# Feed-forward by token group: weights read once for all tokens, or three times in halves

## The chip, the core and the metric

The kernel runs on one core of a Trainium2 chip. The metric is the device time of one execution in microseconds. The kernel before takes 3298.15 us, the median of 3 runs (3295.02 to 3298.2).

A core has five engines that run beside each other, each with its own queue in program order: TensorE (PE, matrix products; its weight loads are shown as PEld), VectorE (DVE), ScalarE (ACT), GpSimd (POOL) and SyncE (SP), which here issues transfers. DMA engines move data between device memory (HBM) and the on-chip memories: SBUF, and PSUM, into which PE writes its sums. Engines wait for each other through semaphores.

## The reference

Two layers of a transformer-like step in float32, for 1024 prompt tokens and 32 sample tokens with 1024 features. Cut to what matters here:

```
def _sq_relu_mlp(h, w_up, w_down):
    return jnp.square(jax.nn.relu(h @ w_up)) @ w_down

for layer in range(2):
    mix = _ab_mixer(...) if layer % 2 == 0 else _s5_mixer(...)
    x = x + _rmsnorm(mix, g[1])
    x = x + _rmsnorm(_cross_attn(_rmsnorm(x, g[2]), ...), g[3])
    h = _rmsnorm(x, g[4])
    x = x + _rmsnorm(_sq_relu_mlp(h, w_up[layer], w_down[layer]), g[5])
```

The feed-forward maps 1024 features to 4096 hidden ones and back. Layer 0 mixes tokens by retention and forgetting attention, layer 1 by an S5 state-space layer, whose input is a product of the normed x with a 1024 x 1024 matrix (`w_in_c`).

## The kernel before, in words

Activations lie feature-major, features on the 128 partitions, tokens along the free axis, in three groups: g0 and g1 of 384 tokens, g2 of 256 + 32 = 288. Each large float32 product runs as three passes in fp32r over splits x = xh + xl and w = wh + wl: wh with xh, wh with xl, wl with xh (`mm3`).

A weight block of 128 x 1024 floats (512 KB) comes through `wload`: SP issues a transfer into a staging tile `wst` (2 buffers), ACT copies it to `wh` (line 139), and DVE subtracts to get `wl` (line 140); `wh` and `wl` have 4 buffers each. A block serves 8 x 3 = 24 products per token group.

The feed-forward (`mlp`) goes over 8 chunks of 512 hidden features. In each chunk four up blocks are loaded and multiplied for g0, g1 and g2 in turn; each result is evacuated (`evac_up`) by ACT (relu, line 1343), DVE (square, line 1344), ACT (high half `ho`, line 1346) and POOL (low half, line 1347). Then four down blocks are loaded and give 8 outputs for each group, summed up over the chunks in `y` by DVE (line 1366). Each weight block is loaded once and serves 72 products. In the last chunk a group's `y` is complete; `done` then starts its `update`: sums of squares (ACT `sq` line 244, POOL `acc` line 245), their sum over partitions by a small product on PE (`c` or `a`), the reciprocal root (`ms`, `rc`, `r`), its spread over partitions by another small product (`b`), and then for each of 8 parts y times gain and root (`upd`, DVE line 273), plus the residual `xr` read back from HBM (line 274, on DVE or POOL), the stored copy `xs`, and the split of the new x for the next product (`xh` ACT line 201, `xl` DVE line 202). The cross-attention's output product before the feed-forward ends in the same `update`.

The order of PE's program is written by hand (`_Order`): `po.later` puts a small product off until enough other products stand before it, and `po.tick` inserts those that are due. The other engines are ordered by a scheduler, with evacuations and put-off pieces at a raised priority; each engine then takes its instructions strictly in that order.

After the feed-forward of layer 0 comes the S5 input product: `gemm` over 8 blocks, the first `gran` of them taken together per token group before the next group, and each finished block goes to `s5_block`, whose first products on PE use a table `Gm`. PSUM has three banks for large products (`mm`).

## Time and profile before

| | |
|---|---|
| median of the runs | 3298.15 us (3295.02 to 3298.2) |
| span of the profiled execution, first to last instruction | 3296.3 us |
| instructions | 50246 |
| PE, PEld, DVE, ACT, POOL busy | 96%, 93%, 45%, 33%, 28% |
| mean granted clock of TensorE | 0.980 |
| DMA | 285.71 MB, mean 87 GB/s |

The profile is of one execution. Its own time is not listed apart from the runs; its span lies 1.9 us below their median. A granted clock of 1.00 is full speed. A matrix product's record is longer than its distance to the next, since products are pipelined: the distance between two starts is what counts.

### The profile page before, as it was taken

Reading aid. Unit: us, or ns where it says so; the run is one execution under the profiler, and the core shown is the slowest. Engines: PE = TensorE matmul, PEld = TensorE weight load, DVE = VectorE, ACT = ScalarE, POOL = GpSimd, SP = SyncE. Lnnn points to the kernel's source line nnn. Section 1 sums busy time; section 2 is a strip of 40 time slices with the busy share of each in tenths; the row PEclk is TensorE's granted clock in tenths of the full one; section 3 lists DMA queues with packets and bytes.
Section 4 is the critical chain, followed back from the end, with each engine's and each line's share of the span. In section 5 each row is a group of like instructions: output and inputs, shape, how many; then the busy total and the mean of one; then the engine's idle time right before and its main releaser. Section 6 shows DMA issues by size and latency. Waiting matters only on the chain.

```text
span 3296.3 us, 50246 instructions
## 1 busy us (share of the span) xinstructions
PE 3160.3 (96%) x19972; PEld 3059.2 (93%) x19972; DVE 1495.2 (45%) x2756; ACT 1071.6 (33%) x2117; POOL 914.5 (28%) x1182
## 2 busy tenths in 40 slices
PE   7999999998999999999999888998999999999997
PEld 7899986688999999999999878998999999999997
DVE  8843566527435223332334797227426132233224
ACT  5212335425435322221124334225435321222212
POOL 4873431216115211111114442015106111111115
PEclk9999999999999999999999998999999999999998
DMA  5562244124114211110112677114124110111113
GB/s 157 156 194 70 62 137 128 38 58 141 52 42 128 65 42 52 52 47 31 52 52 74 204 241 222 57 52 141 49 66 124 52 47 32 52 52 52 39 58 99
DMA packets 176336, 285.71 MB, mean 87 GB/s; under 512 B 34027, under 2 KB 130508, under 8 KB 175972
## 3 DMA queue, kind: packets, MB, share of 16 engines
q1 hardware_dynamic: 132310, 215.02, 21.8%
q10 hardware_dynamic: 35328, 41.83, 3.8%
q0 software_dynamic: 8464, 25.66, 2.3%
q8 instruction: 157, 2.57, 0.3%
q14 instruction: 77, 0.63, 0.1%
HBM read 220.17 MB, written 66.39 MB: 87 GB/s over the span
## 4 chain that ended last, share of the span: by engine, by line
PE 77%; DVE 7%; POOL 6%; DMA 4%; issue 4%; ACT 2%; SPq 0%; DVEq 0%; ACTq 0%; POOLq 0%
PE mm L72 68%; PE a L72 4%; PE b L72 2%; POOL q L527 2%; POOL acc L245 2%; PE c L72 1%; DVE xl L202 1%; DVE wl L140 1%; DVE upd L274 1%; POOL ET L528 1%; DMA ed<-ET 1%; POOL ET L529 1%; DVE upd L273 1%; PE b L76 1%; DMA mt<-in_memt_dram 0%
## 5 line engine op out<-in xcount | busy, mean ns | idle before, releaser
L72 PE MATMUL mm<-xh,wh 128*128 128x384 f32 (+1 forms) x3168 | 1050.4, 332 | 6.5 <-ACT mo L382 3.7
L72 PE MATMUL mm<-xh,wl 128*128 128x384 f32 (+1 forms) x3168 | 1031.4, 326 | 7.4 <-DVE wl L140 7.3
L72 PE MATMUL mm<-xl,wh 128*128 128x384 f32 (+1 forms) x3168 | 1031.9, 326 | 1.2 <-DVE xl L202 1.2
L72 PE MATMUL mm<-ho,wh 128*128 128x384 f32 (+1 forms) x3456 | 822.9, 324 | 1.5 <-DVE y L1366 1.5
L72 PEld LDWEIGHTS mm<-xh,wh 128*128 128x128 f32 x3168 | 603.5, 190 | 13.8 <-issue 5.0
L72 PEld LDWEIGHTS mm<-xh,wl 128*128 128x128 f32 x3168 | 602.4, 190 | 9.0 <-DVE wl L140 9.0
L72 PEld LDWEIGHTS mm<-xl,wh 128*128 128x128 f32 x3168 | 603.5, 190 | 1.8 <-DVE xl L202 1.8
L72 PEld LDWEIGHTS mm<-ho,wh 128*128 128x128 f32 x3456 | 603.5, 188 | 1.8 <-DVE y L1366 1.8
L72 PE MATMUL mm<-ho,wl 128*128 128x384 f32 (+1 forms) x1728 | 558.2, 323 | 0.0
L1347 POOL TENSOR_TENSOR ho<-u,ho 128x384 fp32r<-128x384 f32 (+1 forms) x192 | 183.3, 955 | 1176.2 <-ACT ho L1346 1150.4
L140 DVE TENSOR_TENSOR wl<-wst,wh 128x1024 fp32r<-128x1024 f32 (+1 forms) x252 | 318.5, 1264 | 416.0 <-ACT wh L139 412.8
L139 ACT ACTIVATE wh<-wst 128x1024 fp32r<-128x1024 f32 (+1 forms) x252 | 266.5, 1059 | 708.9 <-PE mm L72 641.6
L245 POOL TENSOR_TENSOR acc<-acc,sq 128x384 f32<-128x384 f32 (+2 forms) x259 | 280.9, 1093 | 412.1 <-ACT sq L244 406.5
L1366 DVE TENSOR_TENSOR y<-y,mm 128x384 f32<-128x384 f32 (+1 forms) x336 | 174.3, 519 | 353.4 <-PE mm L72 353.2
L72 PEld LDWEIGHTS mm<-ho,wl 128*128 128x128 f32 x1728 | 325.5, 188 | 0.0
L1344 DVE TENSOR_TENSOR u<-u 128x384 f32<-128x384 f32 (+1 forms) x192 | 103.3, 538 | 409.7 <-ACT u L1343 409.7
L1343 ACT ACTIVATE u<-mm 128x384 f32<-128x384 f32 (+1 forms) x192 | 88.0, 458 | 313.8 <-PE mm L72 313.6
L1346 ACT ACTIVATE ho<-u 128x384 fp32r<-128x384 f32 (+1 forms) x192 | 95.7, 498 | 172.1 <-DVE u L1344 172.1
L1206 POOL TENSOR_SCALAR p<-p,mx 128x256 f32<-128x256 f32 (+1 forms) x72 | 36.7, 510 | 241.4 <-DVE mx L1205 138.8
L202 DVE SCALAR_TENSOR_TENSOR xl<-upd,gall,xh 128x384 fp32r<-128x384 f32 (+1 forms) x120 | 100.0, 834 | 5.1 <-ACT xh L201 4.8
L244 ACT ACTIVATE sq<-y 128x384 f32<-128x384 f32 (+1 forms) x126 | 61.9, 495 | 109.7 <-DVE y L1366 56.2
L72 PE MATMUL mm<-xo,wh 128*128 128x384 f32 (+1 forms) x384 | 92.1, 324 | 0.0
(427 smaller groups left out, 4132.9 us busy)
## 6 DMA issues: line engine op xcount, KB each, us to landing
wst<-in_wup_dram SPq DMA_DIRECT2D x64, 512.0 KB
wst<-in_wdn_dram SPq DMA_DIRECT2D x64, 512.0 KB
xs<-upd ACTq DMA_DIRECT2D x80, 192.0 KB
xr<-xs SPq DMA_DIRECT2D x80, 192.0 KB
wst<-in_wab_dram SPq DMA_DIRECT2D x20, 512.0 KB
wst<-in_wxk_dram SPq DMA_DIRECT2D x16, 512.0 KB
wst<-in_wxv_dram SPq DMA_DIRECT2D x16, 512.0 KB
wst<-in_wxq_dram SPq DMA_DIRECT2D x16, 512.0 KB
```

The source lines that it names most:

```text
L72: return nc.tensor.matmul(out, lhsT, rhs, **kw)
L139: act(wh[:, :n], st[:, :n], AF.Copy)
L140: vtt(wl[:, :n], st[:, :n], wh[:, :n].bitcast(F32), op=SUB)
L202: stt(l, src, gain, h.bitcast(F32), op0=MULT, op1=SUB)
L244: act(sq[:, :n], src, AF.Square)
L245: return gtt(acc[:, :n], acc[:, :n], sq[:, :n], op=ADD)
L527: gtt(o[:, :, :, :m], ET[:, :, :, :m], a_, op=MULT)
L1343: act(t, ps, AF.Relu)
L1344: vtt(t, t, t, op=MULT)
L1346: act(h, t, AF.Copy)
L1347: gtt(lo, t, h.bitcast(F32), op=SUB)
L1366: vtt(Y[g][o], Y[g][o], ps, op=ADD)
```

## The change

The feed-forward takes the token groups one after the other. For each group it goes over 4 chunks of 1024 hidden features: 8 up blocks, then 8 outputs from 4 pairs of down blocks (8 hidden blocks are summed in PSUM before one evacuation, where it were 4), so `y` is summed up over 4 chunks. Each weight block is loaded once per group, three times in all, and serves 24 products per load. A group's `update` is issued when its own pass is over. PE's products are the same in number and shape.

`wload` stages each block in two halves of 128 x 512 floats (256 KB): two transfers, four half-sized `wst` buffers, two `wh` copies (line 141) and two `wl` subtractions (line 142). This holds for all of the kernel's weights. The S5 input product opens with three blocks instead of two. Comments are left out in the new file, so that line numbers shift (update: 273 becomes 275, 274 becomes 276, `xl` 202 becomes 204, `xh` 201 becomes 203, relu 1343 becomes 1355, square 1344 becomes 1356, the high half, now `hm`, 1346 becomes 1358).

```
@@ wload
-            st = wp.tile([128, 1040], F32, tag="wst", bufs=2, name="wst")
-            dma(st[:, :n], src.rearrange("p k m -> p (k m)"))
             wh = wp.tile([128, 1040], F32R, tag="wh", bufs=4, name="wh")
             wl = wp.tile([128, 1040], F32R, tag="wl", bufs=4, name="wl")
-            with tc.high_priority(offset=offset):
-                act(wh[:, :n], st[:, :n], AF.Copy)
-                vtt(wl[:, :n], st[:, :n], wh[:, :n].bitcast(F32), op=SUB)
+            src = src.rearrange("p k m -> p (k m)")
+            for s in (slice(0, n // 2), slice(n // 2, n)):
+                st = wp.tile([128, 520], F32, tag="wst", bufs=4, name="wst")[:, : n // 2]
+                dma(st, src[:, s])
+                with tc.high_priority(offset=offset):
+                    act(wh[:, s], st, AF.Copy)
+                    vtt(wl[:, s], st, wh[:, s].bitcast(F32), op=SUB)
@@ mlp
-            Y = [[None] * 8 for _ in range(3)]
-            for c in range(8):
-                H = [[None] * 4 for _ in range(3)]
...
-                gemm(range(4), lambda b: wload(A["wup"][l, 4 * c + b], 8, HP if c == 0 and b == 2 else 0), lambda g, k: get(X, g)[k], evac_up, 4)
-                ws = [wload(A["wdn"][l, c, s], 4) for s in range(4)]
-                for g in range(3):
...
+            for g in range(3):
+                n = NG[g]
+                Y, acc = [None] * 8, None
+                x = get(X, g)
+                for c in range(4):
+                    H = [None] * 8
+                    for b in range(8):
+                        wh, wl = wload(A["wup"][l, 8 * c + b], 8)
+                        ps = bank()[:, :n]
+                        for k in range(8):
+                            s = slice(k * 128, k * 128 + 128)
+                            mm3(ps, wh[:, s], wl[:, s], x[k][0], x[k][1], k == 0, k == 7)
                             po.tick()
                         with tc.high_priority(offset=HP):
...
+                            act(t, ps, AF.Relu)
+                            vtt(t, t, t, op=MULT)
+                            h, lo = (hid[0].tile([128, 384], F32R, tag="hab", bufs=16, name="hm")[:, :n] for _ in range(2))
+                            act(h, t, AF.Copy)
+                            gtt(lo, t, h.bitcast(F32), op=SUB)
+                            H[b] = (h, lo)
+                    if c == 3:
+                        acc = acc_tile(n)
+                    for s4 in range(4):
+                        ws = [wload(A["wdn"][l, 2 * c + j, s4], 4) for j in range(2)]
+                        for o in (2 * s4, 2 * s4 + 1):
+                            ps = bank()[:, :n]
+                            for k in range(8):
+                                wh, wl = ws[k // 4]
...
+                                mm3(ps, wh[:, s], wl[:, s], H[k][0], H[k][1], k == 0, k == 7)
+                                po.tick()
+                            with tc.high_priority(offset=HP):
+                                if c == 0:
+                                    Y[o] = ytile(g)
+                                    act(Y[o], ps, AF.Copy)
+                                else:
+                                    vtt(Y[o], Y[o], ps, op=ADD)
+                                if c == 3:
+                                    sumsq(acc, Y[o], n, o == 0, "sqa")
+                done(g, Y, acc)
@@ S5 input product
-        gemm(range(8), ..., evac_u, lambda at: 2 if at == 0 else 1,
+        gemm(range(8), ..., evac_u, lambda at: 3 if at == 0 else 1,
```

The first place is DVE at the entry of layer 0's feed-forward. In the kernel before, `wl_12040` is the low half of up block 1, `wl_12046` that of block 2 (block 0's stands three rows ahead of the first row here), `u_12114` the square of block 0, and `upd`, `xl` and `y` belong to g1's update.

```order
L202 SCALAR_TENSOR_TENSOR xl_12007<-upd_12003,gall_81,xh_12006 128x384
L274 TENSOR_TENSOR upd_12086<-upd_12086,xr_12084 128x384
L273 SCALAR_TENSOR_TENSOR upd_12127<-y_11685,gall_81,b_11928 128x384
L140 TENSOR_TENSOR wl_12040<-wst_12037,wh_12039 128x1024
L202 SCALAR_TENSOR_TENSOR xl_12065<-upd_12061,gall_81,xh_12064 128x384
L212 TENSOR_SCALAR ms_12107<-c_12103 128x3
L274 TENSOR_TENSOR upd_12127<-upd_12127,xr_12125 128x384
L140 TENSOR_TENSOR wl_12046<-wst_12043,wh_12045 128x1024
L202 SCALAR_TENSOR_TENSOR xl_12090<-upd_12086,gall_81,xh_12089 128x384
L273 SCALAR_TENSOR_TENSOR upd_12152<-y_11741,gall_81,b_11928 128x384
L1344 TENSOR_TENSOR u_12114<-u_12114 128x384
```

In the change `wl_12304` is the low half of up block 0, `wl_12380` that of block 1, and `u_12372` the square of block 0; the `upd` and `xl` ahead of it belong to g1's update.

```order
L204 SCALAR_TENSOR_TENSOR xl_12323<-upd_12319,gall_81,xh_12322 128x384
L276 TENSOR_TENSOR upd_12395<-upd_12395,xr_12393 128x384
L275 SCALAR_TENSOR_TENSOR upd_12420<-y_12013,gall_81,b_12200 128x384
L204 SCALAR_TENSOR_TENSOR xl_12348<-upd_12344,gall_81,xh_12347 128x384
L276 TENSOR_TENSOR upd_12420<-upd_12420,xr_12418 128x384
L142 TENSOR_TENSOR wl_12304<-wst_12309,wh_12303 128x512
L204 SCALAR_TENSOR_TENSOR xl_12399<-upd_12395,gall_81,xh_12398 128x384
L204 SCALAR_TENSOR_TENSOR xl_12424<-upd_12420,gall_81,xh_12423 128x384
L214 TENSOR_SCALAR ms_12365<-c_12361 128x3
L1356 TENSOR_TENSOR u_12372<-u_12372 128x384
L142 TENSOR_TENSOR wl_12380<-wst_12381,wh_12379 128x512
L142 TENSOR_TENSOR wl_12380<-wst_12385,wh_12379 128x512
```

Block 0's second half (`wst_12309`) now stands behind the add of g1's seventh part, and block 1's two halves behind block 0's square; before, blocks 1 and 2 stood ahead of that square. Block 0's first half stands nine rows ahead of its second.

The second place is ACT. In the kernel before, `wh_12039` (block 1) and then `wh_12045` (block 2) are made far ahead of block 0's relu `u_12114`; the rows up to that relu are these.

```order
L280 DMA xs113_118<-upd_12061 128x384
L139 ACTIVATE wh_12045<-wst_12043 128x1024
L244 ACTIVATE sq_12069<-upd_12061 128x384
L201 ACTIVATE xh_12089<-upd_12086,gall_81 128x384
L280 DMA xs114_119<-upd_12086 128x384
L244 ACTIVATE sq_12094<-upd_12086 128x384
L1343 ACTIVATE u_12114<-mm_12055 128x384
L201 ACTIVATE xh_12130<-upd_12127,gall_81 128x384
L280 DMA xs115_120<-upd_12127 128x384
```

In the change the high half of block 1, `wh_12379`, comes right behind block 0's relu `u_12372`.

```order
L282 DMA xs116_121<-upd_12420 128x384
L246 ACTIVATE sq_12428<-upd_12420 128x384
L1355 ACTIVATE u_12372<-mm_12313 128x384
L141 ACTIVATE wh_12379<-wst_12381 128x512
L141 ACTIVATE wh_12379<-wst_12385 128x512
L1358 ACTIVATE hm_12375<-u_12372 128x384
L141 ACTIVATE wh_12477<-wst_12479 128x512
L141 ACTIVATE wh_12477<-wst_12483 128x512
```

Block 1's high half moved from ahead of block 0's relu to behind it.

The third place is ACT where layer 0 goes over from g1 to g2. In the kernel before, g1's last parts (`xh_18775`, `xs217`) stand beside g2's first ones, and a weight that stands among them (`wh_19206`) is one of the S5 input product.

```order
L201 ACTIVATE xh_18775<-upd_18772,gall_81 128x384
L280 DMA xs216_145<-upd_18772 128x384
L244 ACTIVATE sq_18780<-upd_18772 128x384
L139 ACTIVATE wh_19206<-wst_19204 128x1024
L201 ACTIVATE xh_18800<-upd_18797,gall_81 128x288
L280 DMA xs220_147<-upd_18797 128x288
L241 ACTIVATE acc_18793<-upd_18797 128x288
L201 ACTIVATE xh_18811<-upd_18808,gall_81 128x384
L280 DMA xs217_146<-upd_18808 128x384
L244 ACTIVATE sq_18816<-upd_18808 128x384
```

In the change `u_18040` is the relu of g2's sixth up block (block 5), `wh_18047` the high half of the seventh (block 6), and `xh_18078` g1's last part.

```order
L1355 ACTIVATE u_18040<-mm_17989 128x288
L203 ACTIVATE xh_18032<-upd_18029,gall_81 128x384
L282 DMA xs216_145<-upd_18029 128x384
L1358 ACTIVATE hm_18043<-u_18040 128x288
L246 ACTIVATE sq_18037<-upd_18029 128x384
L203 ACTIVATE xh_18078<-upd_18075,gall_81 128x384
L282 DMA xs217_146<-upd_18075 128x384
L246 ACTIVATE sq_18083<-upd_18075 128x384
L141 ACTIVATE wh_18047<-wst_18049 128x512
L141 ACTIVATE wh_18047<-wst_18053 128x512
L141 ACTIVATE wh_18102<-wst_18104 128x512
```

The weight of the seventh block stands behind g1's last part and its square.

## Rows read from the trace of the kernel before

**Rows 1.** Busy time by engine, whole span: us, share, instructions.

```profile
PE 3160.3 (96%) x19972; PEld 3059.2 (93%) x19972; DVE 1495.2 (45%) x2756; ACT 1071.6 (33%) x2117; POOL 914.5 (28%) x1182
```

**Rows 2.** Table by stretch: length, busy time of each engine, clock, DMA share, GB/s.

```profile
core 0: us, PE busy (x) PEld busy (x) DVE busy (x) ACT busy (x) POOL busy (x), PEclk, DMA share, GB/s
1045.00:1080.00 35.00, 29.27 (x153) 28.41 (x153) 33.77 (x52) 20.84 (x44) 28.07 (x27) 0.85 0.69 201
1100.00:1780.00 680.00, 680.00 (x4237) 680.00 (x4236) 195.34 (x305) 159.95 (x270) 91.13 (x98) 1.00 0.15 47
1336.00:1345.00 9.00, 9.00 (x62) 9.00 (x61) 4.80 (x7) 2.12 (x2) 0.00 (x0) 1.00 0.47 152
1780.00:1860.00 80.00, 68.93 (x404) 67.97 (x403) 63.15 (x106) 36.46 (x72) 53.69 (x57) 0.87 0.59 180
2505.00:2550.00 45.00, 39.32 (x225) 38.21 (x224) 42.37 (x64) 26.57 (x56) 35.79 (x36) 0.89 0.59 174
```

**Rows 3.** Timeline of PE, layer 0's entry: start, length, operation, idle before and releaser.

```profile
1047.23 0.83 PE L72 MATMUL a<-ones_c,acc 128*128 128x1 f32 x6 [0.92 <-POOL acc L245]
...
1050.39 0.34 PE L72 MATMUL mm<-xh,wh 128*128 128x384 f32 x1
...
1053.86 0.34 PE L72 MATMUL mm<-xh,wl 128*128 128x384 f32 x1
1056.06 0.83 PE L72 MATMUL c<-ones_c,acc 128*128 128x1 f32 x6 [1.86 <-POOL acc L245]
...
1058.06 0.53 PE L72 MATMUL mm<-xl,wh 128*128 128x384 f32 x1
...
1071.45 0.51 PE L72 MATMUL mm<-xh,wl 128*128 128x384 f32 x1 [2.95 <-DVE wl L140]
...
1078.48 0.36 PE L72 MATMUL mm<-xh,wl 128*128 128x384 f32 x1
```

**Rows 4.** Timelines of DVE and ACT, the same entry.

```profile
1049.27 1.21 DVE L140 TENSOR_TENSOR wl<-wst,wh 128x1024 fp32r<-128x1024 f32 x1
1050.40 0.60 DVE L202 SCALAR_TENSOR_TENSOR xl<-upd,gall,xh 128x384 fp32r<-128x384 f32 x1
...
1053.84 1.51 DVE L140 TENSOR_TENSOR wl<-wst,wh 128x1024 fp32r<-128x1024 f32 x1
...
1055.21 1.06 ACT L139 ACTIVATE wh<-wst 128x1024 fp32r<-128x1024 f32 x1 [3.37 <-DMA wst<-in_wup_dram]
...
1058.62 1.36 DVE L202 SCALAR_TENSOR_TENSOR xl<-upd,gall,xh 128x384 fp32r<-128x384 f32 x1
...
1061.29 0.53 ACT L1346 ACTIVATE ho<-u 128x384 fp32r<-128x384 f32 x1 [2.74 <-DVE u L1344]
...
1061.71 0.55 DVE L274 TENSOR_TENSOR upd<-upd,xr 128x384 f32<-128x384 f32 x1
```

**Rows 5.** Timelines of PE, ACT, DVE and POOL, up blocks of 288 columns.

```profile
1472.28 0.29 PE L72 MATMUL mm<-xh,wl 128*128 128x288 f32 x1
...
1473.47 0.29 PE L72 MATMUL mm<-xh,wl 128*128 128x288 f32 x1
...
1474.24 0.39 ACT L1343 ACTIVATE u<-mm 128x288 f32<-128x288 f32 x1
1474.36 1.23 DVE L140 TENSOR_TENSOR wl<-wst,wh 128x1024 fp32r<-128x1024 f32 x1 [1.60 <-ACT wh L139]
...
1476.51 0.81 POOL L1347 TENSOR_TENSOR ho<-u,ho 128x288 fp32r<-128x288 f32 x1 [2.38 <-ACT ho L1346]
```

**Rows 6.** Waits of PE from 1790 to 1860: total us, times, longest.

```profile
PE b L72 <- POOL rc L220: 5.6, 2, 4.4
```

**Rows 7.** Timeline of PE: first S5 input product and first product with Gm.

```profile
1813.24 0.34 PE L72 MATMUL mm<-xh,wh 128*128 128x384 f32 x1
...
1869.99 0.39 PE L72 MATMUL a<-U,Gm 128*128 128x132 f32 x2
```

**Rows 8.** Chain of waits at the end of the kernel: start, length, what.

```profile
3269.56 1.40 POOL xt L274 x2
...
3277.33 1.45 PE c L72 x6
```

More of the change, by code (lines that the diff above doesn't have):

```diff
@@ L1360, in mlp @@
                             po.tick()
                         with tc.high_priority(offset=HP):
-                            if c == 0:
-                                Y[g][o] = ytile(g)
-                                act(Y[g][o], ps, AF.Copy)
-                            else:
-                                vtt(Y[g][o], Y[g][o], ps, op=ADD)
-                            if c == 7:
-                                sumsq(acc, Y[g][o], NG[g], o == 0, "sqa")
-                    if c == 7:
-                        done(g, Y[g], acc)
+                            t = npl.tile([128, 384], F32, tag="tmp", bufs=2, name="u")[:, :n]
@@ new lines, in mlp @@
+                            act(t, ps, AF.Relu)
[12 more added lines that the diff above has]
+                                wh, wl = ws[k // 4]
+                                s = slice((k % 4) * 256 + (o % 2) * 128, (k % 4) * 256 + (o % 2) * 128 + 128)
+                                mm3(ps, wh[:, s], wl[:, s], H[k][0], H[k][1], k == 0, k == 7)
[8 more added lines that the diff above has]
+                                    sumsq(acc, Y[o], n, o == 0, "sqa")
@@ L1513, in _body @@
         close_after(left, X, (0, 1), s5_start)
-        gemm(range(8), lambda b: wload(A["winc"][b], 8, HP if b < 2 else 0), lambda g, k: get(X, g)[k], evac_u, lambda at: 2 if at == 0 else 1,
+        gemm(range(8), lambda b: wload(A["winc"][b], 8, HP if b < 2 else 0), lambda g, k: get(X, g)[k], evac_u, lambda at: 3 if at == 0 else 1,
              post=lambda b, g: s5_block(b, uts.pop(b)) if un[b] == 3 else None, final=(2, 0, 1))
```

16 lines of the change are left out of this document (removed).

## The prediction, made before the change was timed

> **What bounds the kernel now.** I read the busy table first: TensorE (PE) is busy for 3160.3 of 3296.3 us [rows 1], so only a change in its work, its waits or its clock can move the time. The change adds no product and takes none away; what counts is where PE stands still or runs at half speed. The table by stretch comes next [rows 2]. In the long feed-forward stretch of layer 0 PE is busy for 680.00 of 680 us at clock 1.00: nothing can be gained there. Time is lost at three seams. From 1045 to 1080 (entry into layer 0's feed-forward) PE idles 5.73 us and runs at 0.85; with the missing clock charged on its busy time (0.15 x 29.27 = 4.4) that is 10.1 us. From 2505 to 2550 (the same entry in layer 1) it is 5.68 + 0.11 x 39.32 = 10.0 us. From 1780 to 1860 (the last chunk of layer 0 and the S5 input product) it is 11.07 + 0.13 x 68.93 = 20.0 us.
>
> The timeline of PE at the first entry [rows 3] shows how a seam costs. After an idle of 0.92 us the next products still start 0.17 us apart ((1053.86 - 1050.39) / 20 = 0.1735, so a block of 24 products takes 4.16 us with 384 columns; 21 of them cover 3.64 us). After 1.86 us idle the records lengthen, from 1058.06 on, from 0.34 to 0.53 us: the lower of the two clock levels (1.2 of 2.4 GHz). After 2.95 us they are long from 1071.45 to 1078.48, so of those 7 us nearly half, 3.2 us, is lost. The 2.95 us are a wait for `wl`, VectorE's low half of a weight: VectorE (DVE) is busy for 33.77 of the 35 us of this stretch [rows 2], with the norm updates of g1 and g2 in front of the weights.
>
> **Steady feed-forward: 0.** A weight block now serves 24 products, 3.17 us with 288 columns (24 x 0.132, from (1473.47 - 1472.28) / 9 [rows 5]), so the weight stream must triple to 512 KB per 3.2 to 4.2 us, 125 to 165 GB/s. Before already does that in bursts: from 1336 to 1345 PE is busy for 9.00 of 9 us at 152 GB/s, with the DMA engines busy for 0.47 of the time [rows 2]; 165 GB/s would be 0.51. Per block ScalarE (ACT) would need 2 half copies, a relu and a copy, DVE two halves and a square, all below 2.4 us of 3.2 or 4.2.
>
> The halves themselves: a whole `wl` takes 1.21 us and a whole `wh` 1.06 us [rows 4]. A 384-column add takes 0.55 us on DVE and a 384-column copy 0.53 on ACT [rows 4], so a line through the two points gives a 512-column half 0.68 and 0.64 us, two halves 1.36 and 1.28: 0.15 and 0.22 us more per block, beside PE's work in the steady stretches.
>
> **Hand-over from up to down: +2 us, between 0 and 8.** There are 24 of these, 3 groups x 4 chunks x 2 layers. The first down output needs the evacuation of the last up block after 21 products. Before shows that evacuation with 288 columns: relu at 1474.24, square behind a whole `wl`, copy, and POOL done at 1476.51 + 0.81 = 1477.32 [rows 5], 3.08 us. With a half `wl` (0.68 for 1.23) it is about 2.5, and a wait for the product's end and the semaphores come on top, against 2.8 us of cover (21 x 0.132); with 384 columns it is some 0.5 longer against 3.64 us. I take a quarter of a microsecond at the 8 of g2 and nothing at the 16 others; the top is 1 us at each of the 8. [...]
>
> **Entries: +12 us, between -2 and +26 for both.** Before, `wl` of block 0 ran at 1049.27 and of block 1 at 1053.84, with parts of g1's update behind them [rows 4]. The order of the change puts the first half of block 0 two update instructions later, and the second half behind the add of g1's seventh part of eight (the DVE pieces in the section on the change). The first is done at about 1051.4; then come eight instructions of 0.55 to 0.85 us, 6 us, and the half itself: 1058.1. PE, which could start at 1050.4, has used the first half by 1053.6: 4.5 us idle plus 0.9 before it, where before had 1.86. The clock then drops as it did after 2.95 us, 3.2 us, and I take 4 since a second wait follows. Block 1's `wh` stands on ACT behind the relu of block 0 (it was far ahead): relu, half `wh` and half `wl` end before its third product, about 2 us. Block 5 stands in the same way behind block 4 (another 2, plus 1.5 of clock), block 4's second half comes 0.7 late. Sum 0.9 + 4.5 + 4 + 2 + 2 + 1.5 + 0.7 = 15.6, plus the 0.92 that both have, 16.5 against 10.1: +6 each. The cover before was that the `wh` of three blocks stood ahead of block 0's relu. The low end is that the late halves take the place of before's waits altogether; the high end is block 2 or 3 caught as well (3 us and its clock).
>
> **Group switches: +12 us, between +4 and +22.** Before there was no such place: updates of g0 and g1 ran beside the down products of the next group, whose weights were there. Now g0's and g1's updates (8 parts of three instructions of 0.55 to 1.36 us [rows 4], some 16 us of DVE) run beside the first up blocks of the next group. In layer 0 the order puts block 5's second half of `wl` behind g0's whole update, and block 6's `wh` behind g1's whole update and block 5's relu (the ACT pieces of that section). The first is needed 20.8 + 2.1 us after the switch and comes at about 25: 2.5 idle and 1.5 of clock, 4 us. The second is needed at 6 x 3.17 = 19.0 and comes at 24: 5 idle and 2 of clock, 7 us. In layer 1 the last update has no split to make (stt and add alone): 0.5 us at each of its two switches, 1 in all. SP's queue matters too: g1's and g2's residual loads now stand among the weight loads, and one that waits for an update part holds the weights behind it; that is the top end.
>
> **Layer 0 into S5: -12 us, between -5 and -19.** At the end of layer 0 only g2's update is left. Before, PE waited there for POOL's `rc` alone 5.6 us [rows 6], with g1's update in the way. The feed-forward's last product is followed by one of S5's input at 1813.24, and the first `Gm` product starts at 1869.99 [rows 7], 56.8 us later. The change puts 195 products of 384 columns and 96 of 288 between them (165 and 72 before): 195 x 0.1735 + 96 x 0.132 + about 4 for the small ones + 2 of idle (two of three PSUM banks held by g2's evacuations) = 52.5. The 7 or so lost between 1780 and 1813 go as well. That makes 11 to 12. The S5 stage keeps its pace, set by its eight states. At the low end the third block's evacuation, which finds only two `u` buffers, costs 3 us at two groups; the high end is all of the 20.0.
>
> **Tail: -1 us (0 to -3).** POOL's residual adds of g1 (1.40 us at 3269.56) stand among the sums of g2, and the last norm product starts only at 3277.33 [rows 8]. They go; the chain of y, square and sum that is left is 2 us. **Halves elsewhere: 0 us (-4 to +6)**, 124 loads at +0.14, nearly all beside PE, some started earlier where the DMA ends last.
>
> Sum: 0 + 2 + 12 + 12 - 12 - 1 + 0 = +13 us. The profiled span is 3296.3, the median of the runs 3298.15; the 1.9 us around it stay. Forecast 3298.15 + 13 = 3311.
>
> **Rivals.** A, faster: the late half of block 0 takes the place of waits that are there anyway (the 1.86 us for `acc` lies inside it, and block 3, needed later, has its `wl` by then), and PE's short waits behind it keep the clock. Then the entries cost what they did (0), the switches 5, the hand-overs 0, and the S5 seam gives 18 and the tail 2: -15, 3283 us. For it: the 2.95 us at the entry and the 5.6 us at the seam [rows 3, 6] are owed to updates that stand ahead of more urgent work. Against it: each engine takes its instructions in the order printed, and there the second half of `wl` stands behind an update longer than the waits that it could hide. It decides once entries and switches together cost less than 13 us.
>
> B, no measurable change: the entries +6 together, the switches +8, the seam -14, the tail -1, so -1: 3297. For it: both sides rest on the same engine's queue and are of one size.
>
> C, much slower: the staged stream falls behind. The Trainium skill (DMA: Bandwidth & Descriptors, "Measured" and "Anatomy of one DMA") says to batch transfers to at least 1 MiB; these shrink to 256 KB, and by its fixed 2 us and 436 GB/s a half would take an estimated 2.6 us, a block 5.2 if its halves did not overlap, more than the 3.2 to 4.2 it may take. By the rows alone: if the 152 GB/s of the burst [rows 2] is all that the path gives, a block takes 524288 B / 152 GB/s = 3.45 us, 0.28 more than g2's 3.17; at 128 blocks of g2 that is 36 us on top of the sum: 3347. Against it: 0.47 busy in that burst.
>
> **Chances.** Forecast 0.50 (its own range 3304 to 3322), B 0.18, A 0.22, C 0.10. What can be told from no change here is 0.2%, 6.6 us: faster 0.22, same 0.18, slower 0.60. The bounds of the terms add to -24 and +57; 8 in 10 lies between 3283 and 3338.
>
> **What would show it.** In the table by stretch: 100% PE at clock 1.00 between the seams, about 150 GB/s. At the entries a wait for `wl` of 3 us or more some 12 products into the first up block, and waits for `wh` and `wl` at the starts of the second and the sixth; at both layer-0 switches one wait near block 5 or 6. The first `Gm` product should come 52 to 53 us after the last product of the feed-forward instead of 56.8. It is wrong if PE idles a little at each block (C), or if the entries lose no more than 10 us (A).

## The result and the profile after

The changed kernel takes 3358.77 us (median of 4 runs, 3352.57 to 3364.63) against 3298.18 for the kernel before: the ratio is 1.0182, 95% interval 1.0168 to 1.0197. The profiled execution spans 3354.8 us, 58.5 more than the 3296.3 before. The forecast was 3311, its range 3283 to 3338. The kernel is slower as forecast, but by 60.6 us where 13 were forecast: outside the range, and above even the 3355 to which the upper bounds of all terms add up.

The busy table of the kernel after (us, share, instructions):

```profile
PE 3172.4 (95%) x19972; PEld 3061.8 (91%) x19972; DVE 1751.9 (52%) x3328; ACT 1375.5 (41%) x2881; POOL 912.4 (27%) x1182
```

PE is busy for 12 us more than in [rows 1] with the same 19972 products, so part of the loss is time at the lower clock level; the rest is idle. Where it lies is read from the starts of seven products in the timeline of PE, which cut the program into stretches: the first up and the last down product of each layer's feed-forward, the first and the last product with `Gm`, and the first of the GLU stage (the gated product that ends layer 1's mixer). The table is worked out from them (us; each column is one profiled execution):

| stretch | before | after | difference |
|---|---|---|---|
| start to first up product of layer 0 | 1050.4 | 1055.4 | +5.0 |
| feed-forward, layer 0 | 762.7 | 790.8 | +28.1 |
| to the first Gm product | 56.9 | 52.0 | -4.9 |
| first to last Gm product | 131.5 | 130.2 | -1.3 |
| to the GLU stage (keys and values of the memory for layer 1's cross-attention) | 47.9 | 60.7 | +12.8 |
| GLU stage to first up product of layer 1 | 468.6 | 470.1 | +1.6 |
| feed-forward, layer 1 | 756.1 | 774.9 | +18.8 |
| tail | 22.2 | 20.7 | -1.6 |

The table by stretch of the kernel after (columns as in [rows 2]) shows that inside the feed-forward the losses sit where the prediction looked for them, and only there; the 12.8 us at the memory keys and the 5.0 ahead of the feed-forward lie outside it, where the prediction put nothing:

```profile
1055.00:1112.00 57.00, 43.21 (x216) 39.85 (x216) 44.27 (x69) 30.28 (x62) 30.80 (x30) 0.88 0.56 175
1115.00:1345.00 230.00, 230.00 (x1318) 230.00 (x1317) 93.90 (x156) 91.11 (x172) 30.75 (x31) 1.00 0.40 126
1345.00:1395.00 50.00, 44.89 (x255) 44.06 (x254) 36.90 (x55) 26.72 (x54) 24.52 (x22) 0.93 0.53 164
1395.00:1625.00 230.00, 230.00 (x1318) 230.00 (x1317) 93.88 (x156) 91.81 (x173) 30.92 (x31) 1.00 0.39 125
1625.00:1670.00 45.00, 35.35 (x247) 34.42 (x246) 34.59 (x55) 24.80 (x53) 21.52 (x22) 0.89 0.57 176
1670.00:1840.00 170.00, 169.61 (x1276) 168.90 (x1275) 85.41 (x151) 83.84 (x169) 23.21 (x29) 1.00 0.51 164
2559.00:2618.00 59.00, 44.98 (x219) 42.02 (x219) 45.24 (x69) 30.15 (x62) 31.15 (x31) 0.83 0.51 157
```

Between entry and switches PE is busy for 230 of 230 us at 126 and 125 GB/s, and with 288 columns for 169.61 of 170 at 164 GB/s with the DMA engines 0.51 busy: the stream keeps up. The entry (first row, and last row for layer 1) and the two switches (third and fifth) lose time.

Below, an up pass is a group's eight up blocks of one chunk, a down pass its eight outputs. Undisturbed, an up pass of the changed kernel takes 33.5 us with 384 columns and 25.5 with 288, a down pass 33.6 and 25.8.

The waits of PE at the entry of layer 0, from its timeline (in brackets: idle before, and releaser), which answer to [rows 3]:

```profile
1056.66 0.44 PE L72 MATMUL mm<-xh,wl 128*128 128x384 f32 x1 [0.77 <-DVE wl L142]
...
1064.72 0.69 PE L72 MATMUL mm<-xh,wl 128*128 128x384 f32 x1 [5.69 <-DVE wl L142]
...
1070.66 0.69 PE L72 MATMUL mm<-xh,wh 128*128 128x384 f32 x1 [1.10 <-ACT wh L141]
...
1089.25 0.44 PE L72 MATMUL mm<-xh,wl 128*128 128x384 f32 x1 [1.50 <-DVE wl L142]
...
1094.57 0.56 PE L72 MATMUL mm<-xh,wl 128*128 128x384 f32 x1 [2.94 <-DVE wl L142]
...
1099.10 0.44 PE L72 MATMUL mm<-xh,wh 128*128 128x384 f32 x1 [1.10 <-ACT wh L141]
```

These are the places that were named: block 0's two halves, block 1's `wh`, block 4, block 5's `wh`. The records of 0.69 us behind the long wait are products at the lower clock level (the granted clock is 0.50 from 1064.10 to 1074.20); those of 0.44 are the first after a wait of 0.77, 1.50 or 1.10 us at the higher one.

The waits at layer 0's two switches and at the memory keys, from the same timeline:

```profile
1377.12 0.69 PE L72 MATMUL mm<-xh,wh 128*128 128x384 f32 x1 [4.92 <-ACT wh L141]
...
1655.67 0.61 PE L72 MATMUL mm<-xh,wh 128*128 128x288 f32 x1 [8.12 <-ACT wh L141]
...
1994.82 0.58 PE L72 MATMUL mm<-xmh,wh 128*128 128x256 f32 x1 [13.16 <-ACT wh L141]
```

ACT's timeline before the second of them shows why `wh` is late: it stands behind the last square of g1's update.

```profile
1654.09 0.60 ACT L203 ACTIVATE xh<-upd,gall 128x384 fp32r<-128x384 f32 x1
1654.59 0.51 ACT L246 ACTIVATE sq<-upd 128x384 f32<-128x384 f32 x1
1655.01 2.18 ACT L141 ACTIVATE wh<-wst 128x512 fp32r<-128x512 f32 x4
```

### The profile page after: what moved, and what is told of

It is laid out like the page before. It is cut to its first block, busy times and chain, and to the rows that moved or that the text cites. A ratio compares the mean times of both kernels' runs of the same rounds, so it can differ in the third digit from the quotient of the medians.

```text
span 3354.8 us, 54104 instructions
## 1 busy us (share of the span) xinstructions
PE 3172.4 (95%) x19972; PEld 3061.8 (91%) x19972; DVE 1751.9 (52%) x3328; ACT 1375.5 (41%) x2881; POOL 912.4 (27%) x1182
## 4 chain that ended last, share of the span: by engine, by line
PE 77%; DVE 9%; DMA 4%; issue 4%; ACT 3%; POOL 2%; SPq 1%; DVEq 0%; ACTq 0%; POOLq 0%
PE mm L72 68%; PE a L72 4%; PE b L72 2%; PE c L72 1%; DVE wl L142 1%; DVE upd L276 1%; DVE xl L204 1%; DVE upd L275 1%; POOL acc L247 1%; PE b L76 1%; DMA U<-ud 1%; ACT wh L141 1%; DMA wst<-in_wxk_dram 1%; DVE u L1356 0%; DMA wst<-in_wdn_dram 0%
## 5 line engine op out<-in xcount | busy, mean ns | idle before, releaser
L142 DVE TENSOR_TENSOR wl<-wst,wh 128x512 fp32r<-128x512 f32 (+1 forms) x1016 | 702.0, 711 | 777.5 <-ACT wh L141 727.1
L141 ACT ACTIVATE wh<-wst 128x512 fp32r<-128x512 f32 (+1 forms) x1016 | 613.5, 627 | 796.5 <-PE mm L72 701.6
L72 PE MATMUL mm<-hm,wh 128*128 128x384 f32 (+1 forms) x3072 | 730.5, 323 | 4.1 <-ACT hm L1358 1.9
L72 PEld LDWEIGHTS mm<-xh,wh 128*128 128x128 f32 x3168 | 605.0, 191 | 37.5 <-ACT wh L141 20.0
L72 PEld LDWEIGHTS mm<-hm,wh 128*128 128x128 f32 x3072 | 535.1, 188 | 6.9 <-POOL hm L1359 4.4
L72 PE MATMUL mm<-hm,wl 128*128 128x384 f32 (+1 forms) x1536 | 494.9, 322 | 0.0
L1359 POOL TENSOR_TENSOR hm<-u,hm 128x384 fp32r<-128x384 f32 (+1 forms) x192 | 186.1, 970 | 1082.2 <-ACT hm L1358 1082.2
L72 PEld LDWEIGHTS mm<-hm,wl 128*128 128x128 f32 x1536 | 288.2, 188 | 0.0
L1377 DVE TENSOR_TENSOR y<-y,mm 128x384 f32<-128x384 f32 (+1 forms) x144 | 74.9, 520 | 163.6 <-PE mm L72 163.6
L1358 ACT ACTIVATE hm<-u 128x384 fp32r<-128x384 f32 (+1 forms) x192 | 95.7, 499 | 80.9 <-DVE u L1356 80.7
L246 ACT ACTIVATE sq<-y 128x384 f32<-128x384 f32 (+1 forms) x126 | 61.5, 492 | 109.9 <-DVE y L1377 60.9
L203 ACT ACTIVATE xh<-upd,gall 128x384 fp32r<-128x384 f32 (+1 forms) x120 | 69.8, 583 | 60.7 <-DVE upd L276 46.8
```

The source lines that it names most:

```text
L72: return nc.tensor.matmul(out, lhsT, rhs, **kw)
L141: act(wh[:, s], st, AF.Copy)
L142: vtt(wl[:, s], st, wh[:, s].bitcast(F32), op=SUB)
L203: act(h, src, AF.Copy, scale=gain)
L246: act(sq[:, :n], src, AF.Square)
L1358: act(h, t, AF.Copy)
```

## The experiments

The theories: **O**, the order on ACT and DVE puts weights behind updates, and that is the loss at entries and switches; **H**, the halves themselves cost outside the feed-forward; **G**, opening with three blocks costs later in the S5 stage; against O, **S** or **V**: the engines have no time for update and weights at once, in whatever order. Letters that come later are explained in the expectation that uses them. The stretches below are those of the table, against the kernel before.

**e1: halves alone.** The kernel before with the changed `wload`, nothing else.

```
-            st = wp.tile([128, 1040], F32, tag="wst", bufs=2, name="wst")
-            dma(st[:, :n], src.rearrange("p k m -> p (k m)"))
...
+            for s in (slice(0, n // 2), slice(n // 2, n)):
+                st = wp.tile([128, 520], F32, tag="wst", bufs=4, name="wst")[:, : n // 2]
...
```

> The kernel before with one part of the change alone: every weight block staged, copied and subtracted in two halves. The traces of before and after differ outside the feed-forward by +5.0 us up to the first up product (1050.4 to 1055.4) and by +12.8 us between the last Gm product and the first product of the GLU stage (47.9 to 60.7). Theory H (halves): both belong to the staging, so this kernel takes 3298 + 5 + 13, about 3312 to 3318, with the PE wait for wh of some 13 us at the memory keys. Theory G (three blocks opened): only the +5 belongs to the halves, so about 3303, and the memory keys keep their 48 us. The forecast on record put 0 on the halves elsewhere: 3298.

Measured: 3332.45 us, ratio 1.0101 (1.0084 to 1.0118): worse than any theory said. The stretches: +13.9 to the first up product, +8.8 and +8.2 in the feed-forwards, +3.2 at the memory keys. The wait of 13 us is not there, so that part of H falls. But the entry now shows the waits of the changed kernel, although all groups still share a weight (timeline of PE in e1):

```profile
1065.60 0.45 PE L72 MATMUL mm<-xh,wl 128*128 128x384 f32 x1 [0.78 <-DVE wl L142]
...
1073.64 0.69 PE L72 MATMUL mm<-xh,wl 128*128 128x384 f32 x1 [5.66 <-DVE wl L142]
...
1079.59 0.69 PE L72 MATMUL mm<-xh,wh 128*128 128x384 f32 x1 [1.10 <-ACT wh L141]
```

DVE's timeline in e1 has the two halves of block 0 with eight instructions of g1's update between them:

```profile
1064.63 0.92 DVE L142 TENSOR_TENSOR wl<-wst,wh 128x512 fp32r<-128x512 f32 x1
...
1072.11 1.48 DVE L142 TENSOR_TENSOR wl<-wst,wh 128x512 fp32r<-128x512 f32 x1
```

A weight in two pieces gives the scheduler room to put update parts between them, and the product needs both. In e1 the third block keeps the raised priority that `mlp` gives it before, and the change drops; the waits come all the same.

**e2: three opening blocks alone.**

```
-        gemm(range(8), ..., evac_u, lambda at: 2 if at == 0 else 1,
+        gemm(range(8), ..., evac_u, lambda at: 3 if at == 0 else 1,
```

> The kernel before with one part of the change alone: the S5 input product opens with three blocks. Theory G: PE spends its spare products earlier, so it runs out of them behind the last Gm product, +13 us there, and the first Gm product comes 4 to 8 us later after the feed-forward: 3306 to 3318. Theory H: the end of the S5 stage is paced by its states, so nothing is lost: 3296 to 3302, stretch from last Gm to the GLU stage 48 us.

Measured: 3319.77 us, ratio 1.0063 (1.0048 to 1.0078). +7.1 us to the first Gm product, +4.7 to the last, +7.3 behind it: theory G. The longest wait of PE from 1810 to 2060 (total, times, longest) is the one for `wh` at the memory keys, with whole blocks:

```profile
PE mm L72 <- ACT wh L139: 15.2, 1, 15.2
```

PE has spent its spare products of the S5 input earlier and gets to the memory keys before their weights, whose loads stand on SP behind the S5 stage's own (timeline of SP in e2; PE's wait ends at 1984.37):

```profile
1976.56 0.34 SPq L1445 DMA_DIRECT2D ud<-u  x1
1977.00 1.28 SPq L348 DMA_DIRECT2D mt<-in_memt_dram  x2
1978.34 0.95 SPq L135 DMA_DIRECT2D wst<-in_wxk_dram  x2
```

**e3: the changed kernel with whole blocks** (`wload` of before).

```
-            for s in (slice(0, n // 2), slice(n // 2, n)):
-                st = wp.tile([128, 520], F32, tag="wst", bufs=4, name="wst")[:, : n // 2]
...
+            st = wp.tile([128, 1040], F32, tag="wst", bufs=2, name="wst")
+            dma(st[:, :n], src.rearrange("p k m -> p (k m)"))
...
```

> The changed kernel with whole blocks staged, as before; groups one by one and three opening blocks are kept. Theory H: the 18 us lost outside the feed-forward come back, entries and switches stay within 5 us: 3336 to 3344. Theory G: only the 5 us before the feed-forward come back: about 3353. If halves also caused the losses at the entries (24 us over before) and switches (33 us), it would fall below 3325.

Measured: 3377.99 us, ratio 1.0233 (1.0216 to 1.0251): slower than the changed kernel, against all three expectations. Outside, 8.5 us come back before the feed-forward and 5.8 at the memory keys, but the feed-forwards take 36.4 and 32.4 us more than before. Each down pass of 384 columns takes 34.3 us (33.6 in the changed kernel), of 288 columns 26.8 (25.8). The reason is in the waits of PE over the whole span of e3:

```profile
PE mm L72 <- POOL hm L1357: 12.1, 23, 1.2
...
PE mm L72 <- ACT hm L1356: 6.3, 8, 2.6
```

In the changed kernel the first of them is this:

```profile
PE mm L72 <- POOL hm L1359: 1.4, 3, 0.6
```

So the halves pay at the hand-overs from up to down and cost outside.

The entries do not get better with whole blocks: their first up passes take 58.7 and 58.9 us, as in the changed kernel (57.4 and 58.9). Block 0's low half is there in time now, but PE waits at blocks 2 and 3, longest for block 3's `wh`, which stands on ACT behind the whole update of g2 (timelines of ACT and PE in e3):

```profile
1075.76 0.44 ACT L244 ACTIVATE sq<-upd 128x288 f32<-128x288 f32 x1
1076.11 1.99 ACT L139 ACTIVATE wh<-wst 128x1024 fp32r<-128x1024 f32 x2
...
1077.20 0.69 PE L72 MATMUL mm<-xh,wh 128*128 128x384 f32 x1 [6.63 <-ACT wh L139]
```

So the halves alone are enough for the loss at the entries (e1), and taking them away is not enough to end it.

**e4: the order turned round.** The changed kernel, up weights of a group's first chunk above the update's priority.

```
-                        wh, wl = wload(A["wup"][l, 8 * c + b], 8)
+                        wh, wl = wload(A["wup"][l, 8 * c + b], 8, 2 * HP if c == 0 else 0)
```

> The changed kernel with one number changed: the copies and subtractions of the up weights of a group's first chunk get a priority above that of the norm update, so that on ACT and DVE they stand ahead of it (block 6 of g2 right behind block 1's evacuation, where it stood behind g1's last part). Theory O (order): the waits for wh of 4.9 and 8.1 us at layer 0's switches go, of the 10.9 us for wl at each entry most go, with the half clock behind them: 35 to 50 us less, 3310 to 3325. Rival S (rate: the weight stream, or DVE and ACT together, cannot serve update and weights in that time): the updates now hold up PE instead, within 10 us of the changed kernel, 3349 to 3362.

Measured: 3354.63 us, ratio 1.0177 (1.016 to 1.0194), level with the changed kernel (1.0168 to 1.0197): theory O as it stood falls, and S is closer. The waits for weights at the entry and at the first switch are gone, but PE waits for the update's sums in their place (entry; then first switch):

```profile
1062.11 0.83 PE L72 MATMUL c<-ones_c,acc 128*128 128x1 f32 x6 [2.48 <-POOL acc L247]
...
1079.12 0.83 PE L72 MATMUL a<-ones_c,acc 128*128 128x1 f32 x6 [3.43 <-POOL acc L247]
...
1094.56 1.44 PE L72 MATMUL a<-ones_c,acc 128*128 128x1 f32 x6 [2.92 <-POOL acc L247]
...
1377.49 1.44 PE L72 MATMUL a<-ones_c,acc 128*128 128x1 f32 x6 [5.81 <-POOL acc L247]
```

PE's order is fixed: a sum that nobody needs for long still stops it where it is written. At the second switch the wait goes over to the first down weight, whose priority was not raised:

```profile
1655.22 0.85 PE L72 MATMUL mm<-hm,wh 128*128 128x288 f32 x2 [5.61 <-ACT wh L141]
```

**e5: that sum later.** e4 with `pre_scale` put off by 13 instead of 5.1 in the updates around the feed-forward (`l3=13` at both calls).

```
-                        po.later(L3, lambda: pre_scale(acc2))
+                        po.later(l3, lambda: pre_scale(acc2))
```

> The kernel of e4 (up weights of a group's first chunk ahead of the norm update on ACT and DVE) with one more number: the small product that sums the squares of the new x (a) is put off by 13 instead of 5.1 us of products in the updates around the feed-forward. In e4 PE waited 27.5 us for POOL's acc before that product, at entries and switches. Theory W (the wait moved): the update needs its time on DVE, ACT and POOL in any case, and in e4 PE's fixed order ran into its sum instead of the weights; with the sum later in PE's order the wait goes, 15 to 25 us less than e4: 3328 to 3340. Rival S (the engines cannot keep up): something else in the update or the weights behind it is waited for, within 8 us of e4's 3354.6: 3346 to 3362.

Measured: 3343.74 us, ratio 1.0131 (1.0116 to 1.0147), 11 us less than e4: between the ranges of the two theories. The waits for `a` at entry and switch go; the first up passes shrink from 52.3 to 49.1 and from 45.3 to 34.8 us, but the down passes behind them grow from 33.6 to 39.4 and 42.1. The profiled executions (3345.6 and 3347.6) differ by only 2 us: e4's is the shortest of its four, e5's one of the two longer ones. So the gain rests on the medians, and the traces do not show where it lies.

**e6: the changed kernel with two opening blocks.**

```
-        gemm(range(8), ..., evac_u, lambda at: 3 if at == 0 else 1,
+        gemm(range(8), ..., evac_u, lambda at: 2 if at == 0 else 1,
```

> The changed kernel with two opening blocks in the S5 input product, as before. Theory G (three blocks cost, as in e2 alone: +7.1 us to the first Gm product, +4.7 between the first and last, +7.3 behind the last): the same 15 to 20 us come back: 3339 to 3345. Theory H (in the changed kernel those places are set by the halves on SP's queue): at most 7 us come back, those to the first Gm product: 3350 to 3358.

Measured: 3347.15 us, ratio 1.0134 (1.0116 to 1.0152), between the ranges of the two theories. The stretch to the GLU stage falls from 60.7 to 51.5, that to the first Gm product from 52.0 to 49.3: 9 of the 12.8 us belong to the three blocks, 3.6 to the halves.

**e7: halves in the feed-forward alone,** two transfers and conversions into one whole `wst` tile, two such tiles; whole blocks elsewhere.

```
-            for s in (slice(0, n // 2), slice(n // 2, n)):
-                st = wp.tile([128, 520], F32, tag="wst", bufs=4, name="wst")[:, : n // 2]
+            st = wp.tile([128, 1040], F32, tag="wst", bufs=2, name="wst")
+            for i in range(parts):
+                s = slice(i * n // parts, (i + 1) * n // parts)
...
-                        wh, wl = wload(A["wup"][l, 8 * c + b], 8)
+                        wh, wl = wload(A["wup"][l, 8 * c + b], 8, 0, 2)
...
-                        ws = [wload(A["wdn"][l, 2 * c + j, s4], 4) for j in range(2)]
+                        ws = [wload(A["wdn"][l, 2 * c + j, s4], 4, 0, 2) for j in range(2)]
```

> The changed kernel with halves in the feed-forward alone (two transfers, copies and subtractions into one whole staging tile, two such tiles); every other weight is staged whole as before. Theory H: the stretches outside the feed-forward go back to e3's, 8 us less up to the first up product and 6 less between last Gm and GLU; the hand-overs stay at the changed kernel's (33.6 us per down pass of 384 columns, where e3 had 34.3): 3342 to 3347. Rival: the hand-overs owe their speed to four separate staging tiles, so the down passes go back to 34.3 and 26.8: 3358 to 3368.

Measured: 3359.97 us, ratio 1.018 (1.0165 to 1.0195): no gain. The time lies in the rival's range, but its mechanism is not there: the down passes stay at 33.5 and 25.8 us, so halved conversions, not four tiles, serve the hand-over. The stretch before the feed-forward is back at 1049.5, but that to the last Gm product grows by 4.8 over before. Against the changed kernel the down passes behind layer 1's two switches are 4.9 us longer together, those behind the two entries 2.4.

**e8: all causes together** (e7 with priority for up and first down weights, late sum, two opening blocks).

```
-                        wh, wl = wload(A["wup"][l, 8 * c + b], 8, 0, 2)
+                        wh, wl = wload(A["wup"][l, 8 * c + b], 8, 2 * HP if c == 0 else 0, 2)
...
-                        ws = [wload(A["wdn"][l, 2 * c + j, s4], 4, 0, 2) for j in range(2)]
+                        ws = [wload(A["wdn"][l, 2 * c + j, s4], 4, 2 * HP if c == 0 and s4 == 0 else 0, 2) for j in range(2)]
...
-                        po.later(L3, lambda: pre_scale(acc2))
+                        po.later(l3, lambda: pre_scale(acc2))
...
-        gemm(range(8), ..., evac_u, lambda at: 3 if at == 0 else 1,
+        gemm(range(8), ..., evac_u, lambda at: 2 if at == 0 else 1,
```

> All of it together: groups one by one; halves in the feed-forward alone; the weights of a group's first chunk (up, and the first pair of down) ahead of the update; the sum a put off by 13 us; two opening blocks. If the causes add up (feed-forward of layer 0 at about 770 us and of layer 1 at 758, first Gm product some 45 us behind it, the rest as before): 3285 to 3300, so level with the kernel before or a little under it. If the update's cost only moves again: above 3312.

Measured: 3314.08 us, ratio 1.0047 (1.0032 to 1.0062): 45 us less than the changed kernel, but above the range of "adds up" and in that of "the cost only moves" (above 3312). All stretches outside the feed-forward are level with the kernel before or below it (to the first Gm product -7.6). What is left is 21.6 and 10.5 us in the feed-forwards, over entries and switches, in waits spread over relu, `hm` and the sums. No version here beats the kernel before.

**e9: the update spread.** The changed kernel, the distance between an update's parts made 6.3 for the updates behind the passes (`pu=6.3`; 1.7 for g0, 1.6 for g1 otherwise).

```
-                        po.later(PU[g], lambda: part(k + 1))
+                        po.later(pu or PU[g], lambda: part(k + 1))
```

> The changed kernel with one number: the eight parts of the update behind a group's feed-forward pass are issued 6.3 us of products apart instead of 1.7, so that they lie beside some 50 us of products, not 14. Theory D (the update is packed too close: DVE, ACT and POOL serve weights, evacuations and update of one group within the next group's first blocks): the losses at the four switches (10.1, 13.8 with its down pass 1.1, and in layer 1 4.2 and 3.6 us over an undisturbed pass) fall to under a third, 20 us or more in all: 3333 to 3341. Rival Q (a queue, not load: what holds the weights is one late instruction, and spreading only moves it): 3350 to 3362. The entries are not touched and keep some 24 us each.

Measured: 3361.4 us, ratio 1.0189 (1.0173 to 1.0205). The edit does not do what it was meant to: the parts still run in a block. A likely reason is that their raised priority reaches further than they were put off; no run shows it. DVE's timeline has the first and the last low half but one of g1's update as close as before:

```profile
1639.20 0.71 DVE L204 SCALAR_TENSOR_TENSOR xl<-upd,gall,xh 128x384 fp32r<-128x384 f32 x1 [0.73 <-ACT xh L203]
...
1653.66 0.61 DVE L204 SCALAR_TENSOR_TENSOR xl<-upd,gall,xh 128x384 fp32r<-128x384 f32 x1
```

It leaves theory D open and says nothing against it.

**e10 and e11: e8 with the spread,** 6.3 behind the passes and 3.2 at the entry, and e11 with `c` at the entry put off by 9 too.

```
-            X = proj_out(8, ..., gi + 3, xscr(p), xscr(p + 1), l3=13)
+            X = proj_out(8, ..., gi + 3, xscr(p), xscr(p + 1), l3=13, pu=3.2)
...
-                update(out[g], g, ..., l3=13)
+                update(out[g], g, ..., l3=13, pu=6.3)
```

```
-            po.later(L1, post_scale)
+            po.later(l1, post_scale)
```

> The kernel of e8 with the updates spread: 6.3 us between the parts behind the feed-forward passes, 3.2 us in the update that the feed-forward opens with. Theory D: the 24 us that e8 still loses at its switches (10 and 14 in layer 0, 1 and 5 in layer 1) shrink to under 10; the entries keep the 6 us wait for POOL's acc before c: 3296 to 3304. Rival Q: 3310 to 3318.

> The kernel of e10 with the sum c of the update at the entry put off by 9 instead of 3.2 us of products, since e8 waited 6.3 and 6.9 us for POOL's acc there, in each layer. Theory W: these waits and the half clock behind them go, 8 to 14 us less than e10: 3284 to 3294, under the kernel before. Rival: the chain behind c (root, spread, update of g2) is needed in time, and its delay holds the next thing: within 4 us of e10.

Measured: 3325.78 (1.0075 to 1.0115) and 3330.47 us (1.0085 to 1.0115), both slower than e8 and above the ranges of D, Q and W. In e10 the first up passes at the entry fall to 47.6 and 47.7 us, but the down passes behind them rise to 41.7 (35.3 and 33.7 in e8): the wait moves once more. In e11 PE waits for `c` at layer 0's entry for 2.65 us instead of 6.84, but then 2.19 and 2.27 us for `xh` and `xl` of an update. At the switches the parts are not spread here either: the eight low halves of g1's update in layer 0 start within 21.4 us in e10 and 19.3 in e8, where 6.3 us from part to part would make 44. So theory D stays untested.

**e12: the update lighter.** The changed kernel without seven of eight squares and sums in the updates of g0 and g1 in layer 0.

```
-                        sumsq(acc2, t, n, k == 0)
+                        if not lean or k == 0:
+                            sumsq(acc2, t, n, k == 0)
```

> The changed kernel with a part of the work left out: in the updates behind g0's and g1's feed-forward passes in layer 0, seven of the eight squares of the new x on ACT and their sums on POOL are not made (so the next norm's root of these groups is not the reference's). The stores, the splits and everything on DVE stay. Theory P: DVE's own 16 us of update would fit under the next group's first six blocks (19 us); what makes it late is POOL beside it (the squares of the evacuation, u, take 0.45 to 1.27 us there) and ACT's squares ahead of wh. Then the switches of layer 0 lose under 10 us instead of 24 (undisturbed passes: 33.5 and 25.5 us): 3340 to 3348. Theory V: DVE's 16 us alone, in front of the weights, hold them up; the loss stays above 17 us: 3352 to 3362. Layer 1's switches are as before in either case.

Measured: 3342.24 us, ratio 1.0136 (1.0118 to 1.0154), as theory P said. The first up passes behind the switches take 37.5 and 31.3 us instead of 43.6 and 39.3 (33.5 and 25.5 undisturbed): together 9.8 us over undisturbed ones where the changed kernel's are 23.9 over, and the waits for `wh` of 4.92 and 8.12 us are gone. DVE's eight low halves of g1's update (shortest, median and longest ns) in the changed kernel:

```profile
L204 DVE SCALAR_TENSOR_TENSOR xl<-upd,gall,xh x8: 605/659/1373, 1638.1 to 1654.7; 128x384 fp32r<-128x384 f32 x8
```

and in e12:

```profile
L204 DVE SCALAR_TENSOR_TENSOR xl<-upd,gall,xh x8: 603/608/717, 1627.6 to 1639.2; 128x384 fp32r<-128x384 f32 x8
```

The same eight take 11.6 us from first to last instead of 16.6. Two things went at once, ACT's squares and POOL's sums; DVE's records tell what POOL's part is. In the changed kernel's trace 24 of the 96 `xl` of 128x384 have no POOL instruction beside them; none of these took over 0.62 us, though 17 had ACT busy beside them. Every longer one overlaps an instruction of POOL, as the `xl` here does, while the `upd` of line 275 beside POOL keeps its 0.60 (timelines of DVE and POOL in the changed kernel):

```profile
1641.87 0.60 DVE L275 SCALAR_TENSOR_TENSOR upd<-y,gall,b 128x384 f32<-128x384 f32 x1
1642.03 0.82 POOL L1359 TENSOR_TENSOR hm<-u,hm 128x288 fp32r<-128x288 f32 x1 [0.87 <-ACT hm L1358]
...
1643.02 1.13 POOL L247 TENSOR_TENSOR acc<-acc,sq 128x384 f32<-128x384 f32 x1 [0.17 <-ACT sq L246]
1643.19 1.37 DVE L204 SCALAR_TENSOR_TENSOR xl<-upd,gall,xh 128x384 fp32r<-128x384 f32 x1
```

DVE's 22 instructions of g1's update and the four squares among them took 20.3 us in the changed kernel and 15.0 in e12. These 5.3 us are nearly all of the 5.8 by which that stretch of DVE got shorter (20.4 to 14.6).

## Why the prediction was wrong, point by point

- **Steady feed-forward, 0:** right. 230.00 of 230 us, and at 288 columns the DMA share of 0.51 that was worked out. The halves take 0.69 us on DVE and 0.63 on ACT, as worked out (0.68 and 0.64; the 0.14 more per load that the term on halves elsewhere uses fits neither of its own 0.15 and 0.22).
- **Hand-over, +2:** right, at about 3. The down passes of 384 columns take 33.56 us, as before; those of 288 take 25.84 against 25.48 for an up pass, 0.37 at each of eight. That the halves make it so (e3: 34.3 and 26.8) was the reason given.
- **Entries, +12:** mis-sized. The first up passes lose 24 and 25 us over an undisturbed 33.5; before, the up products of the first chunk lost 12.6 in each layer over an undisturbed 46.3: +11 and +13. The mechanism is the one named, block by block; block 4 was put at 0.7 us and waits 1.50 + 2.94, block 0's second half 4.5 and waits 5.69, and DVE's xl and add took up to 1.37 us where 0.55 to 0.85 stood in the sum. e1 shows that the halves alone bring it about, e3 that whole blocks lose as much, at blocks 2 and 3. The change also drops the raised priority of the third block's weight; no run gives that back alone, but with a raised priority for all eight (e4) the first up passes still take 52.3 and 53.7 us.
- **Group switches, +12:** the step that failed most. They cost 10.1 and 13.8 + 1.1 us in layer 0 and 7.7 in layer 1, 33 together, above the term's upper bound of 22. The prediction let g1's update end, and the seventh block's weight come, 24 us behind the switch, with 16 us of DVE's parts in front. The parts did sum to 16 us, but the first started 9.5 us behind the switch, and the squares of the evacuations among them, which the sum left out, took 4.2 us (1.8 in e12, without POOL's sums): 20.3 us of DVE work. So the weight came 29 us behind the switch (1655.01, with g2's first up product at 1626.10), not 24. In layer 1 the cost was put at 1 us from the count of instructions alone.

```profile
1626.10 0.29 PE L72 MATMUL mm<-xh,wh 128*128 128x288 f32 x1
...
1635.65 1.66 DVE L275 SCALAR_TENSOR_TENSOR upd<-y,gall,b 128x384 f32<-128x384 f32 x3
```

- **Layer 0 into S5, -12:** right: 9.8 us of the last chunk and 4.9 to the first Gm product (51.85 us from the first product of the S5 input, forecast 52 to 53), 14.7 in all. With two opening blocks it comes 2.7 us earlier still (e6).
- **S5 stage "keeps its pace" and halves elsewhere, 0:** the second step that failed. That eight states set the pace was said without a row for it. The third opening block is not free behind the first Gm product: 9 of the 12.8 us at the memory keys are its (e2, e6), the other 3.6 the halves'. All traces agree on this stretch: 46.7 to 48.0 us with two blocks and whole weights there, 51.1 and 51.5 with halves, 54.8 to 57.0 with three blocks, 59.7 to 61.5 with both. The halves also cost the time before the feed-forward, but one execution does not show how much: five kernels with the same code up to there took 1050.9 to 1056.5 us. On average over seven traces each it is 1056.7 with halves and 1049.2 without. A split weight is a split place in the queue, which the sum of durations does not show.
- **Tail, -1:** -1.6, and 2.7 more in the last chunk of layer 1. Together the terms give some 3 + 24 + 33 - 15 + 13 + 5 - 4 = 59 us, the 58.5 between the profiled executions.
- Rival C stood near the time (3347) but for the wrong reason: the stream keeps up between the seams, at up to 164 GB/s with PE busy for 169.61 of 170 us. The Trainium skill's rule of 1 MiB (DMA: Bandwidth & Descriptors, "Measured") is one for reaching 75% of the peak. No run here asks for the peak: 256 KB at a time gave the 164 GB/s that were needed, a block of g2 every 3.2 us where the estimate without overlap was 5.2. (The page measured transfers issued from GpSimd; these are issued from SP.) A and B fell with entries and switches, which together cost 57 us.

Not settled: what the dropped priority of the third block's weight costs by itself; whether updates that are really spread would help (theory D); what part ACT's squares have in the switch beside POOL's slowing of DVE; and what makes e7's down passes behind entries and layer 1's switches longer.

## What to carry to other kernels

Work that is moved beside other work is priced by the queue it joins, not by its own length: write down each instruction between the last moment that the data can come and the one that needs it, at the length that it has beside its neighbours. Where one engine's order is fixed by hand, a wait that is taken from one place turns up at the next fixed instruction, as from `wh` to `a` to the down passes here. And a filler that is spent early is missing later: follow it to the end of its stage.

## What the runs showed of the hardware

DVE's `xl` of 128x384 took at most 0.62 us wherever no POOL instruction ran beside it (207 in the 14 traces of this case), and up to 1.44 us beside one (913). It reads two tensors from SBUF, `upd` and `xh`. The `upd` of line 275, of the same shape, reads `y` from SBUF and `b` from PSUM (written there by PE; no transfer of this kernel goes to PSUM); in the changed kernel's trace all 61 that ran beside POOL stayed at 0.62 us or below. The Trainium skill (Advanced Engine Details and Errata, "GPSIMD Details") says that POOL shares a read and a write interface with DVE, in conflict with DVE's instructions that read two tensors from SBUF. The trace agrees with it in both kinds.

After an idle of 0.77 us at the entry the clock level held; after 5.69 us the records are 0.52 to 0.69 us long where 0.34 is the length at the higher level, and the granted clock is 0.50. Short idles close together were followed by the lower level as well: in e7 three of 0.63, 0.95 and 0.63 us, and a granted clock of 0.50 behind them (timeline of PE, then the table by stretch):

```profile
2890.05 0.44 PE L72 MATMUL mm<-hm,wh 128*128 128x384 f32 x1 [0.63 <-POOL hm L1360]
...
2891.62 0.44 PE L72 MATMUL mm<-hm,wh 128*128 128x384 f32 x1 [0.95 <-ACT hm L1359]
...
2892.69 0.69 PE L72 MATMUL mm<-hm,wh 128*128 128x384 f32 x1 [0.63 <-POOL hm L1360]
...
2892.50:2895.80 3.30, 3.11 (x10) 3.11 (x11) 0.00 (x0) 0.49 (x1) 0.14 (x1) 0.50 0.44 159
```
